# Another pool for a weight block, fewer eviction halves and other queues for some rows in a hybrid SSD and attention step

## The chip, the cores and the metric

The kernel runs on one core of a Trainium2 chip. The metric is the device time of one execution in microseconds (us); lower is better. A core has five engines: TensorE (PE in the profile, its weight loads PEld), VectorE (DVE), ScalarE (ACT), GpSimd (POOL, "Pool" below) and SyncE (SP), which here only issues DMAs. SP, ScalarE and Pool each have a queue of their own for the DMAs that they issue; each engine takes its instructions in order, so an instruction that waits holds all that stand behind it on that engine.

## The reference

One step of a one-layer decoder for 512 prompt tokens and 64 sample tokens (8 x 8). All matrices are float32.

```python
# h = rmsnorm(x); one input projection of h gives z, x/B/C, dt, q, k, v, ga, mix_s, mix_a
# attention:  o = sink_attention(q, k, v, rel_bias, window 128) * silu(ga)
# SSD:        y = grouped_rmsnorm(ssd(silu(conv(xBC)), dt) * silu(z))
# merge:      m = sigmoid(mix_s) * (y @ w_ssm) + sigmoid(mix_a) * (o @ w_attn)
# trunk:      out = final_rmsnorm(x + m @ w_out)
```

x has 576 rows of 2048, y has 4096 columns. The new caches of k and v (the old rows moved up by eight, and the new ones), the convolution's state and the SSM state are outputs too.

## The kernel before

Activations stand transposed, a tile of 128 features by T = 576 tokens, in two halves of TH = 288. Each float32 product is made as three products of rounded parts: `ah` and `al` are the high and low part of an activation, `wh` and `wl` those of a weight. A weight block is 128 x 8 x 128 (512 KB, "raw"); ScalarE rounds it to `wh` (L80) and VectorE takes the difference `wl` (L81).

**Two ways of multiplying.** `run_main` makes *single tiles*: 128 output columns from all sixteen feature tiles, two raw blocks each, loaded at L73. `pairs_of` makes *pairs* of output tiles by seven products instead of eight (Strassen's scheme in Winograd's form). Each pair takes four raw blocks (A11, A21, A22, A12, loaded at L380), and VectorE forms S1 = A21 + A22, S2 = S1 - A11, S3 = A11 - A21 and S4 = A12 - S2 out of them (L393). Each product is 24 matmuls of 288 columns. VectorE combines the products (L404) and names the halves p1, u, w, o, c.

**Stages** in the trace before: to about 122 us the norm, the transposes and the first six single tiles; in their shadow `sums_job` forms the combinations T of the activations that the products need. Then the paired run of 22 pairs for the gate columns (ga, z) to about 610, attention to about 1390, SSD to about 2335, the three *branch* products (w_attn, and w_ssm in two parts) to about 2975, and w_out. Each branch product is four single tiles (run_main), while `forms_job` loads the branch's rows once more and forms their combinations, and then six pairs. `merge_out` multiplies each half by its gate row `sg` (L1341 load, L1345 product) and stores it to `mg_d` by Pool (L1352 plain, L1350 adding to what is there).

**Pools in SBUF.** `wp` holds the raw blocks of single tiles, and of pairs A11 and A21, in two buffers. `rs` holds A22, A12, S1 and S2 in five buffers, and the staged rows ("stg") of `acts_in` and `forms_job`. `ev` holds halves of 128 x 288 (tag e), N_E = 14 of them: the halves of products, sums, gate rows, and `x` tiles.

**T1.** The combination T1 (x[0, 0] in `sums_job`) is needed in the buffers `b12`, which the first single tiles still read. So eight halves of `ev` keep it (the list t1) from `sums_job` until the first pair, when `t1_there` splits them into `b12`. At a branch T1 goes to the scratch `xb_d` (L1324) and is loaded from it (L1389) when the single tiles are issued.

**Order.** A scheduler places instructions on each engine by a simulated timeline, and a buffer of a pool is free for its next tile when the last reader of that one buffer is done. SP issues nearly all loads; Pool stores T1, b12 (`xb_d`) and `mg_d`, copies the two caches from DRAM to DRAM in `copy_job` (L529, eight DMAs of 480 KB), and writes the bias for attention to DRAM (L491, 16 DMAs of 383 KB). `acts_in` loads the rows for the single tiles of the next branch (L1309, on SP) and splits them (L1169 ScalarE, L1170 VectorE); `on_products` calls it during the last pair of a branch.

Of the kernel before, what the change touches and what calls it, by code (L numbers as in the profile page):

```python
# [16 lines left out]
P = 128  # L17
# [14 lines left out]
WIN = 128  # L32
EPS = 1e-6
NEG = -1e30
OFF_XBC = DI
OFF_DT = OFF_XBC + CONV
OFF_Q = OFF_DT + H
OFF_K = OFF_Q + D
OFF_V = OFF_K + KVW
# [13 lines left out]

Z_PAIRED = 28
FIRST_OUT = 4
N_E = 14
N_C = 18
N_K = 19

# [26 lines left out]
def hybrid(ctx, tc, x_prompt, x_sample, cache_k, cache_v, state_conv, state_ssm, norm_w, w_in, conv_w,  # L86
# [24 lines left out]
    def scratch(shape, name):  # L111
        return dram.tile(shape, F32, tag=name, name=name)
# [9 lines left out]
    ga_d = scratch([D, T], "ga_d")  # L122
    xb_d = scratch([D // 2, TH], "xb_d")
    mg_d = scratch([D, T], "mg_d")
    oh_d = scratch([HEADS * BL], "oh_d")
    ea_d = scratch([H, T], "ea_d")
    nacs_d = scratch([H, T], "nacs_d")
# [180 lines left out]
    def drain():  # L308
        while quick or jobs:
            pump()  # L310
# [55 lines left out]
    def pairs_of(w, r0, cols, ops, takes, after):  # L366

        n = len(cols)
        st = [{} for _ in cols]

        def load(p, *names):
            for x in names if p < n else ():
                c, kh = cols[p] + P * (x in ("A21", "A22")), x in ("A12", "A22")
                t_ = (rs if kh else wp).tile([P, 8, P], F32, tag="rs" if kh else "raw", name="raw",
                                             bufs=5 if kh else 2)
                sync.dma_start(out=t_, in_=w[r0 + 1024 * kh:r0 + 1024 * kh + 1024, c:c + P].rearrange("(k p) n -> p k n", p=P))  # L380
                st[p][x] = t_

        def sum_(p, x):
            if p >= n:
                return
            s_ = st[p]
            if x in ("S1", "S2"):
                s_[x] = rs.tile([P, 8, P], F32, tag="rs", name="raw", bufs=5)
            else:
                s_[x] = s_["A21" if x == "S3" else "S2"]  # L390
            a, b, op = {"S1": ("A21", "A22", ALU.add), "S2": ("S1", "A11", ALU.subtract),
                        "S3": ("A11", "A21", ALU.subtract), "S4": ("A12", "S2", ALU.subtract)}[x]
            vec.tensor_tensor(out=s_[x], in0=s_[a], in1=s_[b], op=op)  # L393

        def split(p, i):
            if p < n:
                st[p][i] = W.split(st[p][("A11", "S2", "S1", "S3", "A12", "S4", "A22")[i]])

        def evict(p, i):
            s_, (one, two) = st[p], takes[p]  # L400
            ps = s_["ps", i][:, :TH]

            def add(o, b):
                vec.tensor_tensor(out=o, in0=ps, in1=b, op=ALU.add)  # L404
                return o

            if i == 0:
                s_["p1"] = etile("p1")
                act.activation(s_["p1"], ps, AF.Copy)
            elif i == 1:  # L410
                s_["u"] = add(etile("u"), s_["p1"])
            elif i == 2:
                s_["w"] = add(etile("w"), s_["u"])
            elif i == 3:
                two(1, add(s_["w"], s_["w"]), s_["w"])
            elif i == 4:
                one(0, ps, etile("o"))
            else:
                c = add(etile("c"), s_["u"])
                (one if i == 5 else two)(1 if i == 5 else 0, c, c)  # L420

        def head():
            load(0, "A11", "A21", "A22", "A12")
            split(0, 0)
            sum_(0, "S1")
            sum_(0, "S2")
            split(0, 1)
            sum_(0, "S3")

        def run():  # L430
            for p in range(n):
                for i in range(7):
                    if i < 5:
                        split(p, i + 2)
                    else:
                        split(p + 1, i - 5)
                    if i == 1:
                        load(p + 1, "A11", "A21", "A22")
                    elif i == 2:
                        sum_(p, "S4")  # L440
                    elif i == 3:
                        sum_(p + 1, "S1")
                        load(p + 1, "A12")
                    elif i == 4:
                        sum_(p + 1, "S2")
                    elif i == 5:
                        sum_(p + 1, "S3")
                    st[p]["ps", i] = p1.tile([P, 512], F32, tag=f"ps{i}", name="ps") if i < 4 else st[p]["ps", (0, 2, 3)[i - 4]]
                    wh, wl = st[p].pop(i)
                    for k in range(8):  # L450
                        ah, al = ops[i][k]
                        for q, (a, b) in enumerate(((wh, ah), (wh, al), (wl, ah))):
                            ten.matmul(st[p]["ps", i][:, :TH], a[:, k, :], b, start=i < 4 and k == 0 and q == 0,  # L453
                                       stop=k == 7 and q == 2, skip_group_check=i >= 4)
                        pump()
                    evict(p, i)
                    after(p - n, i)

        return head, run
# [690 lines left out]
    def etile(name):  # L1150
        return ev.tile([P, TH], F32, tag="e", name=name)

    hx = [[[hb[k // 8][j][k % 8][part] for j in range(2)] for part in range(2)] for k in range(KT)]


    def pair_pools():
        stk = ExitStack()
        return (stk, *(stk.enter_context(tc.tile_pool(name=n_, bufs=b_, reuse_waits="tile"))
                       for n_, b_ in (("tx", 1), ("rs", 5), ("ev", N_E))))

    stk, tx, rs, ev = pair_pools()
    b12, t1 = hb[0][1], []
    ops = [hb[0][0], [], [], [], hb[1][0], hb[1][1], []]

    def tpair(tag):
# [7 lines left out]
    def sums_job():  # L1173

        yield from wait(36)
        for k in range(8):
            x = {}
            for i, j in ((0, 0), (0, 1), (1, 1), (1, 0)):
                x[i, j] = ev.tile([P, TH], F32, tag="e", name="x")
                vec.tensor_tensor(out=x[i, j], in0=hb[i][j][k][0], in1=hb[i][j][k][1], op=ALU.add)  # L1180
            pool.dma_start(out=xb_d[k * P:(k + 1) * P, :], in_=x[0, 1])
            for o_, a, b in (((0, 0), (0, 1), (0, 0)), ((0, 1), (1, 1), (0, 1)), ((1, 1), (1, 1), (0, 0)),
                             ((1, 0), (1, 0), (1, 1))):
                vec.tensor_tensor(out=x[o_], in0=x[a], in1=x[b], op=ALU.subtract)
                yield
            t1.append(x[0, 0])
            for i, o_ in ((3, (0, 1)), (1, (1, 1)), (6, (1, 0))):
                ops[i].append(split_half(tpair(f"t{i}{k}"), x[o_]))
                yield
# [6 lines left out]
            takes.append([gate_out(AF.Silu, dst, n + u) for u in range(2)])  # L1196
    back = []

    def t1_there():

        for k in range(8):
            split_half(b12[k], t1[k])

    def b12_again(p, i):
        if (p, i) == (-len(cols), 0):
            t1_there()
        elif (p, i) == (-1, 1):
            for k in range(8):
                back.append(etile("x"))
                sync.dma_start(out=back[k], in_=xb_d[k * P:(k + 1) * P, :])  # L1210
        elif (p, i) == (-1, 2):
            for k in range(8):
                split_half(b12[k], back[k])
# [3 lines left out]
    quick.append(sums_job())  # L1217
    run_main([m_in(c, by_halves(gate_out(AF.Sigmoid, d_, n))) for c, d_, n in mixes[:FIRST]], first, then=head)
    drain()
    ms.close()  # L1220
    ms = ExitStack()
    p1 = ms.enter_context(tc.tile_pool(name="p1", bufs=1, space=PSUM, reuse_waits="tile"))
# [53 lines left out]
    left = [m_in(n * P, take_gate(AF.Silu, z_d, n)) for n in range(Z_PAIRED, DI // P)] + left  # L1276
    seq = []
    for g in range(G):
        seq.append(m_in(OFF_XBC + (32 + g) * P, take_conv(32 + g)))
        seq.append(m_in(OFF_XBC + (40 + g) * P, take_conv(40 + g)))  # L1280
        for t in range(4):
            seq.append(m_in(OFF_XBC + (4 * g + t) * P, take_conv(4 * g + t) if t < 3 else last_x(g)))
        seq += left[:MIXES_S[g]]
        del left[:MIXES_S[g]]
    seq += left
# [15 lines left out]
    run_main([m_in(c, by_halves(gate_out(AF.Sigmoid, d_, n))) for c, d_, n in ends], raws=raws)  # L1301

    def staged_rows():
        return rs.tile([P, 8, P], F32, tag="rs", name="stg", bufs=5).rearrange("p a b -> p (a b)")

    def acts_in(src, ks):
        for k in ks:
            t_ = staged_rows()
            sync.dma_start(out=t_[:, :T], in_=src[k * P:(k + 1) * P, :])  # L1309
            split_half(hk[k], t_[:, :T])  # L1310

    tt = [[tpair(f"t{i}{k}") for k in range(8)] for i in (1, 3, 6)]
# [1 line left out]
    def forms_job(src):  # L1314

        for k in range(8):
# [4 lines left out]
            sync.dma_start(out=u2, in_=src[k * P:(k + 1) * P, TH:])  # L1321
            sync.dma_start(out=v[:, :T], in_=src[1024 + k * P:1024 + (k + 1) * P, :])
            vec.tensor_tensor(out=t1_, in0=u2, in1=u1, op=ALU.subtract)
            pool.dma_start(out=xb_d[k * P:(k + 1) * P, :], in_=t1_)  # L1324
            vec.tensor_tensor(out=t2_, in0=v2, in1=t1_, op=ALU.subtract)
            yield
            split_half(tt[0][k], t2_)
# [52 lines left out]
    for i in range(3):  # L1380
# [4 lines left out]
        def last_chunk():  # L1385
            head()
            for k in range(8):
                t1.append(etile("x"))
                sync.dma_start(out=t1[k], in_=xb_d[k * P:(k + 1) * P, :])  # L1389

        head, run = pairs_of(w, r0, [n * P for n in range(FIRST_OUT, KT, 2)], ops,
                             [takes[n:n + 2] for n in range(FIRST_OUT, KT, 2)],
# [157 lines left out]
```

## Time and profile before

| | us |
|---|---|
| median of 3 runs | 3226.87 (3225.44 to 3229.58) |
| the profiled execution | 3228.93 |
| its span, first to last instruction | 3226.8 |
| mean granted TensorE clock in it | 0.983 |

The costliest groups, by line: three matmul groups at L345 (single tiles and the rest of the run through `run_main`) of 1012 to 1021 us each, three at L453 (pairs) of 382 to 384 us each, VectorE's L81 with 728.0 us in 586 instructions, ScalarE's L80 with 620.1 us in as many.

How to read the lines below: a row of a timeline is the start in us, the duration, the engine, line, operation, out<-in by the program's names, and in brackets how long the engine had stood idle before, and what ended that. A row of the waits is who waited for whom: us in total, times, the longest. SPq is SP's own sequence of DMA issues. Names have no buffer numbers in the profile, so `t1_d` would read `t_d`.

### The profile page before, as it was taken

Reading aid. Unit: us, or ns where it says so; the run is one execution under the profiler, and the core shown is the slowest. Engines: PE = TensorE matmul, PEld = TensorE weight load, DVE = VectorE, ACT = ScalarE, POOL = GpSimd, SP = SyncE. Lnnn points to the kernel's source line nnn. Section 1 sums busy time; section 2 is a strip of 40 time slices with the busy share of each in tenths; the row PEclk is TensorE's granted clock in tenths of the full one; section 3 lists DMA queues with packets and bytes.
Section 4 is the critical chain, followed back from the end, with each engine's and each line's share of the span. In section 5 each row is a group of like instructions: output and inputs, shape, how many; then the busy total and the mean of one; then the engine's idle time right before and its main releaser. Section 6 shows DMA issues by size and latency. Waiting matters only on the chain. (4 is left out here: it accounts for less than half of the span.)

```text
span 3226.8 us, 58215 instructions
## 1 busy us (share of the span) xinstructions
PE 3112.4 (96%) x22939; PEld 2993.4 (93%) x22939; DVE 1996.5 (62%) x3434; ACT 1473.7 (46%) x2761; POOL 482.5 (15%) x591
## 2 busy tenths in 40 slices
PE   6989999999999999999999999999999999999997
PEld 5989999999898998999999999998899989998997
DVE  6656666515444443477687687686657777877354
ACT  5434444423554554455555555565433433434333
POOL 3200000000001010112213212212221031311111
PEclk9999999999999999999999999999999999999999
DMA  6564444433343243364464564565575676967655
GB/s 198 143 156 121 122 123 125 117 89 90 84 121 93 82 123 100 100 165 135 135 179 128 147 166 132 148 166 146 147 234 175 194 212 143 249 159 194 180 161 158
DMA packets 733650, 471.18 MB, mean 146 GB/s; under 512 B 45433, under 2 KB 696969, under 8 KB 733185
## 3 DMA queue, kind: packets, MB, share of 16 engines
q1 hardware_dynamic: 691616, 420.51, 46.6%
q0 software_dynamic: 24336, 29.20, 4.4%
q10 hardware_dynamic: 17424, 17.76, 1.7%
q8 instruction: 180, 2.95, 0.4%
q14 instruction: 94, 0.76, 0.1%
HBM read 385.79 MB, written 91.81 MB: 148 GB/s over the span
## 5 line engine op out<-in xcount | busy, mean ns | idle before, releaser
L80 ACT ACTIVATE wh<-raw 128x1024 fp32r<-128x1024 f32 x586 | 620.1, 1058 | 1031.6 <-PE ps L453 488.4
L81 DVE TENSOR_TENSOR wl<-raw,wh 128x1024 fp32r<-128x1024 f32 x586 | 728.0, 1243 | 529.9 <-ACT wh L80 525.9
L345 PE MATMUL ps<-ah,wh 128*128 128x288 f32 (+2 forms) x4384 | 1021.4, 302 | 34.8 <-ACT craw L828 10.1
L345 PE MATMUL ps<-ah,wl 128*128 128x288 f32 (+2 forms) x4384 | 1012.6, 301 | 3.5 <-DVE wl L81 3.3
L345 PE MATMUL ps<-al,wh 128*128 128x288 f32 (+2 forms) x4384 | 1012.4, 300 | 2.5 <-DVE al L1170 2.5
L345 PEld LDWEIGHTS ps<-ah,wh 128*128 128x128 f32 x4384 | 735.2, 192 | 50.5 <-issue 11.1
L345 PEld LDWEIGHTS ps<-ah,wl 128*128 128x128 f32 x4384 | 734.5, 191 | 19.6 <-issue 10.6
L345 PEld LDWEIGHTS ps<-al,wh 128*128 128x128 f32 x4384 | 734.6, 191 | 9.0 <-DVE al L1170 4.1
L453 PE MATMUL ps<-ah,wh 128*128 128x288 f32 x1280 | 382.2, 299 | 13.8 <-DVE w L404 5.6
L453 PE MATMUL ps<-ah,wl 128*128 128x288 f32 x1280 | 383.5, 300 | 5.9 <-DVE wl L81 5.4
L453 PE MATMUL ps<-al,wh 128*128 128x288 f32 x1280 | 381.8, 298 | 0.0
L453 PEld LDWEIGHTS ps<-ah,wh 128*128 128x128 f32 x1280 | 244.4, 191 | 14.7 <-issue 5.8
L393 DVE TENSOR_TENSOR raw<-raw 128x1024 f32<-128x1024 f32 x160 | 194.8, 1220 | 97.6 <-DMA raw<-in_w_in_dram 40.6
L453 PEld LDWEIGHTS ps<-ah,wl 128*128 128x128 f32 x1280 | 244.6, 191 | 9.3 <-DVE wl L81 9.2
L453 PEld LDWEIGHTS ps<-al,wh 128*128 128x128 f32 x1280 | 244.7, 191 | 0.1
L844 DVE SCALAR_TENSOR_TENSOR cacc<-craw,prm,cacc 128x600 f32<-128x600 f32 x144 | 126.8, 885 | 45.4 <-ACT cacc L842 43.7
L882 ACT ACTIVATE L<-L,nacs_n 128x128 f32<-128x128 f32 (+1 forms) x320 | 96.7, 379 | 56.6 <-DVE L L879 56.1
L610 DVE CUSTOM_DVE_ANT_0 sc<-bank,bm 128x256 f32<-128x256 f32 (+1 forms) x128 | 43.8, 388 | 80.0 <-PE bank L606 72.1
L923 POOL TENSOR_TENSOR xl<-xe,xh 128x512 fp32r<-128x512 f32 x32 | 58.6, 1832 | 200.3 <-ACT xh L922 199.9
L879 DVE TENSOR_TENSOR L<-L,nacs_n 128x512 f32<-128x512 f32 (+1 forms) x80 | 51.9, 662 | 47.7 <-DMA L<-nacs_d 47.3
L1093 DVE SCALAR_TENSOR_TENSOR s<-s,dec_s,bank 128x128 f32<-128x128 f32 x256 | 70.4, 340 | 10.3 <-PE bank L1087 9.3
L1241 POOL DMA_DIRECT2D dska<-in_d_skip_dram x1 | 0.6, 586 | 455.9 <-DMA z_d<-c 455.9
(575 smaller groups left out, 4497.7 us busy)
## 6 DMA issues: line engine op xcount, KB each, us to landing
raw<-in_w_in_dram SPq DMA_DIRECT2D x306, 512.0 KB
raw<-in_w_ssm_branch_dram SPq DMA_DIRECT2D x64, 512.0 KB
raw<-in_w_out_dram SPq DMA_DIRECT2D x64, 512.0 KB
L<-nacs_d SPq DMA_DIRECT2D x64, 256.0 KB
s<-in_state_ssm_dram SPq DMA_DIRECT2D x64, 256.0 KB
out_dram<-s SPq DMA_DIRECT2D x64, 256.0 KB
raw<-in_w_attn_branch_dram SPq DMA_DIRECT2D x32, 512.0 KB
stg<-y_d SPq DMA_DIRECT2D x48, 288.0 KB
```

The lines of the kernel that those rows point to most:

```text
L80: pin(nc.scalar.activation(wh, raw, AF.Copy))
L81: pin(nc.vector.tensor_tensor(out=wl, in0=raw, in1=wh, op=ALU.subtract))
L345: ten.matmul(sums[i][:, s, :part.shape[1]], a[:, kk, :], part, start=(k == 0 and q == 0), stop=(k == last and q == 2))
L393: vec.tensor_tensor(out=s_[x], in0=s_[a], in1=s_[b], op=op)
L453: ten.matmul(st[p]["ps", i][:, :TH], a[:, k, :], b, start=i < 4 and k == 0 and q == 0, stop=k == 7 and q == 2, skip_group_check=i >= 4)
L610: vec.tensor_tensor_reduce(out=s_[:, i, lo:256], in0=ps[:, i, lo:256], in1=bm[j][:, i, lo:256], scale=1.0, scalar=-3e38, op0=ALU.add, op1= ...
L844: vec.scalar_tensor_tensor(out=acc[:, :600], in0=raw[:, i:i + 600], scalar=prm[:, i * 48 + j:i * 48 + j + 1], in1=acc[:, :600], op0=ALU.mu ...
L879: vec.tensor_tensor(out=l_[:rows, :, :n], in0=l_[:rows, :, :n], in1=nacs_n[:rows, blk, h:h + 4].unsqueeze(2).to_broadcast([rows, 4, n]), o ...
L882: act.activation(l_[:rows, i, :n], l_[:rows, i, :n], AF.Exp, scale=-1.0, bias=nacs_n[:rows, blk, h + i:h + i + 1])
L923: pool.tensor_tensor(out=xl, in0=xe, in1=xh, op=ALU.subtract)
L1093: vec.scalar_tensor_tensor(out=sts[i][:, t, :], in0=sts[i][:, t, :], scalar=dec_s[:, 4 * g + t, b:b + 1], in1=ps[:, v, i, :], op0=ALU.mult ...
L1241: pool.dma_start(out=dska, in_=AP(d_skip, 0, [[0, P], [1, H]]))
```

## The change

1. A21 moves from the pool `wp` to `rs`, which gets a sixth buffer (5 to 6), through a helper `weights_tile`. `wp` keeps two buffers, for A11 and the single tiles. The loads for the next pair are written in the order A21, A22, A11 instead of A11, A21, A22.
2. `ev` shrinks from 14 halves to 11.
3. T1 of the first stage is stored to a new scratch `t1_d` by Pool and loaded into eight `ev` halves by SP after the first single tiles; the branches use `t1_d` too, instead of `xb_d`.
4. `acts_in` issues its loads from Pool's queue instead of SP's.

A renamed constant (OFF_XBC) has no effect. Lines shift by one to four (L1181 becomes L1184, L1309 L1313, L1341 L1345, L1350 L1354, L1352 L1356).

```diff
-N_E = 14
+N_E = 11
...
+    t1_d = scratch([D // 2, TH], "t1_d")
...
                 c, kh = cols[p] + P * (x in ("A21", "A22")), x in ("A12", "A22")
-                t_ = (rs if kh else wp).tile([P, 8, P], F32, tag="rs" if kh else "raw", name="raw",
-                                             bufs=5 if kh else 2)
+                t_ = weights_tile() if x != "A11" else wp.tile([P, 8, P], F32, tag="raw", name="raw", bufs=2)
...
             if x in ("S1", "S2"):
-                s_[x] = rs.tile([P, 8, P], F32, tag="rs", name="raw", bufs=5)
+                s_[x] = weights_tile()
...
                     if i == 1:
-                        load(p + 1, "A11", "A21", "A22")
+                        load(p + 1, "A21", "A22", "A11")
...
+    def weights_tile(name="raw"):
+        return rs.tile([P, 8, P], F32, tag="rs", name=name)
...
-                       for n_, b_ in (("tx", 1), ("rs", 5), ("ev", N_E))))
+                       for n_, b_ in (("tx", 1), ("rs", 6), ("ev", N_E))))
...
-            t1.append(x[0, 0])
+            pool.dma_start(out=t1_d[k * P:(k + 1) * P, :], in_=x[0, 0])
...
         if (p, i) == (-len(cols), 0):
-            t1_there()
+            for k in range(8):
+                split_half(b12[k], t1[k])
...
     drain()
+    for k in range(8):
+        t1.append(etile("x"))
+        sync.dma_start(out=t1[k], in_=t1_d[k * P:(k + 1) * P, :])
...
     def staged_rows():
-        return rs.tile([P, 8, P], F32, tag="rs", name="stg", bufs=5).rearrange("p a b -> p (a b)")
+        return weights_tile("stg").rearrange("p a b -> p (a b)")
...
             t_ = staged_rows()
-            sync.dma_start(out=t_[:, :T], in_=src[k * P:(k + 1) * P, :])
+            pool.dma_start(out=t_[:, :T], in_=src[k * P:(k + 1) * P, :])
...
-            pool.dma_start(out=xb_d[k * P:(k + 1) * P, :], in_=t1_)
+            pool.dma_start(out=t1_d[k * P:(k + 1) * P, :], in_=t1_)
...
-                sync.dma_start(out=t1[k], in_=xb_d[k * P:(k + 1) * P, :])
+                sync.dma_start(out=t1[k], in_=t1_d[k * P:(k + 1) * P, :])
```

**Pool's queue in the first stage.** Before, with the stores of `sums_job` (xb_d) and the copies of the caches (L529):

```order
24 L1181 DMA xb_d<-x 128x288
25 L1251 DMA sinks_s<-sink_d 64x4x1 x2
26 L529 DMA out_dram<-in_cache_k_dram 2x4x15360 x4
27 L529 DMA out_dram<-in_cache_v_dram 2x4x15360 x4
28 L1181 DMA xb_d<-x 128x288 x7
```

After, from the same place (t_d is t1_d), and then the rows that follow the writes of the bias:

```order
21 L1184 DMA xb_d<-x 128x288
22 L1189 DMA t_d<-x 128x288
23 L1184 DMA xb_d<-x 128x288
24 L1189 DMA t_d<-x 128x288
25 L1184 DMA xb_d<-x 128x288 x2
```

```order
41 L491 DMA bias_d<-oh_d 256x1x383 x16
42 L1245 DMA dska<-in_d_skip_dram 128x64
43 L1250 DMA sk<-in_attn_sinks_dram 32x1
44 L1247 COPY dsk<-dska 64x32 x2
45 L1252 COPY sk_6644<-sk 32x8
46 L1253 DMA sink_d<-sk_6644 32x8
47 L1255 DMA sinks_s<-sink_d 64x4x1 x2
48 L529 DMA out_dram<-in_cache_k_dram 2x4x15360 x4
49 L529 DMA out_dram<-in_cache_v_dram 2x4x15360 x4
```

The eight copies moved from behind the first xb_d store to behind dska, whose load waited until 633.28 us in the trace before; stores of T1 alternate with the other seven.

**SP's queue at the first pairs.** Before: raw_1259 to raw_1265 are A11, A21, A22 and A12 of pair 0 (the last two stand further ahead), raw_1448, 1450, 1452 and 1526 those of pair 1, raw_1690, 1692, 1694 and 1761 those of pair 2:

```order
23 L380 DMA raw_1259<-in_w_in_dram 128x8x128
24 L380 DMA raw_1261<-in_w_in_dram 128x8x128
25 L380 DMA raw_1452<-in_w_in_dram 128x8x128
26 L380 DMA raw_1448<-in_w_in_dram 128x8x128
27 L380 DMA raw_1450<-in_w_in_dram 128x8x128
28 L380 DMA raw_1526<-in_w_in_dram 128x8x128
29 L380 DMA raw_1694<-in_w_in_dram 128x8x128
```

After: raw_1268 is A11 of pair 0 (its other three stand ahead); raw_1473, 1475, 1477 and 1551 are A21, A22, A11 and A12 of pair 1, raw_1715 and 1719 A21 and A11 of pair 2, and raw_1954 A11 of pair 3. Between the two pieces stand the eight loads of T1 (L1223):

```order
22 L380 DMA raw_1268<-in_w_in_dram 128x8x128
23 L380 DMA raw_1473<-in_w_in_dram 128x8x128
24 L380 DMA raw_1477<-in_w_in_dram 128x8x128
25 L380 DMA raw_1719<-in_w_in_dram 128x8x128
```

```order
34 L380 DMA raw_1475<-in_w_in_dram 128x8x128
35 L380 DMA raw_1551<-in_w_in_dram 128x8x128
36 L380 DMA raw_1715<-in_w_in_dram 128x8x128
37 L380 DMA raw_1954<-in_w_in_dram 128x8x128
```

A22 of the next pair, which stood ahead of that pair's A11 and A21, is now the last of the four but A12; A11 stands two pairs ahead, and A21 of the pair after next stands right behind A12.

**Pool's queue at the end of the second branch.** Before, the last stores of the pairs and then the first of the forms:

```order
368 L1350 DMA mg_d<-w 128x288
369 L1350 DMA mg_d<-o 128x288
370 L1350 DMA mg_d<-c 128x288 x2
371 L1350 DMA mg_d<-w 128x288
372 L1350 DMA mg_d<-o 128x288
373 L1350 DMA mg_d<-c 128x288 x2
374 L1324 DMA xb_d<-stg 128x288
```

After, the same two pairs; L1313 are the rows for the next single tiles:

```order
384 L1313 DMA stg<-y_d 128x576
385 L1354 DMA mg_d<-w 128x288
386 L1354 DMA mg_d<-o 128x288
387 L1354 DMA mg_d<-c 128x288
388 L1313 DMA stg<-y_d 128x576
389 L1354 DMA mg_d<-c 128x288
390 L1313 DMA stg<-y_d 128x576 x7
391 L1354 DMA mg_d<-w 128x288
392 L1313 DMA stg<-y_d 128x576 x3
393 L1354 DMA mg_d<-o 128x288
394 L1313 DMA stg<-y_d 128x576 x4
395 L1354 DMA mg_d<-c 128x288 x2
```

Sixteen loads of rows stand between the stores of the last two pairs, fourteen of them around the last pair's, and none behind the last two stores. Ahead of w_out twelve of fourteen stand behind the last store.

More of the change, by code (lines that the diff above doesn't have):

```diff
@@ L34 @@
 NEG = -1e30
-OFF_XBC = DI
-OFF_DT = OFF_XBC + CONV
+OFF_xb_dC = DI
+OFF_DT = OFF_xb_dC + CONV
 OFF_Q = OFF_DT + H
@@ L1158, in pair_pools @@
         return (stk, *(stk.enter_context(tc.tile_pool(name=n_, bufs=b_, reuse_waits="tile"))
-                       for n_, b_ in (("tx", 1), ("rs", 5), ("ev", N_E))))
+                       for n_, b_ in (("tx", 1), ("rs", 6), ("ev", N_E))))
     stk, tx, rs, ev = pair_pools()
-    b12, t1 = hb[0][1], []
+    b12 = hb[0][1]
     ops = [hb[0][0], [], [], [], hb[1][0], hb[1][1], []]
@@ L1197, in hybrid @@
     back = []
-    def t1_there():
-        for k in range(8):
-            split_half(b12[k], t1[k])
+    t1 = []
     def b12_again(p, i):
         if (p, i) == (-len(cols), 0):
-            t1_there()
+            for k in range(8):
+                split_half(b12[k], t1[k])
         elif (p, i) == (-1, 1):
@@ L1278, in hybrid @@
     for g in range(G):
-        seq.append(m_in(OFF_XBC + (32 + g) * P, take_conv(32 + g)))
-        seq.append(m_in(OFF_XBC + (40 + g) * P, take_conv(40 + g)))
+        seq.append(m_in(OFF_xb_dC + (32 + g) * P, take_conv(32 + g)))
+        seq.append(m_in(OFF_xb_dC + (40 + g) * P, take_conv(40 + g)))
         for t in range(4):
-            seq.append(m_in(OFF_XBC + (4 * g + t) * P, take_conv(4 * g + t) if t < 3 else last_x(g)))
+            seq.append(m_in(OFF_xb_dC + (4 * g + t) * P, take_conv(4 * g + t) if t < 3 else last_x(g)))
         seq += left[:MIXES_S[g]]
```

## The prediction

> **What bounds the kernel now.** I read the page first, then the 25 us windows of the whole run, then the lists of waits and the timelines of those windows in which the matmuls fall short. The page says that TensorE is the bound nearly everywhere:
>
> ```profile
> PE 3112.4 (96%) x22939; PEld 2993.4 (93%) x22939; DVE 1996.5 (62%) x3434; ACT 1473.7 (46%) x2761; POOL 482.5 (15%) x591
> ```
>
> So a change that alters no matmul can win only where TensorE waits or runs at a low clock. The windows show where that is: x after PE is the matmuls that fell into the window, PEclk the granted clock, DMA the share of the 16 engines. The windows that matter:
>
> ```profile
> core 0: us, PE busy (x) PEld busy (x) DVE busy (x) ACT busy (x) POOL busy (x), PEclk, DMA share, GB/s
> 25.00:50.00 25.00, 23.61 (x156) 20.91 (x154) 22.88 (x57) 15.86 (x35) 13.60 (x15) 1.00 0.55 154
> 50.00:75.00 25.00, 19.55 (x128) 18.12 (x129) 17.49 (x46) 12.81 (x30) 1.71 (x3) 0.93 0.57 181
> 75.00:100.00 25.00, 25.00 (x190) 25.00 (x189) 19.75 (x45) 9.54 (x20) 2.16 (x4) 1.00 0.46 133
> 100.00:125.00 25.00, 25.00 (x190) 25.00 (x189) 17.21 (x29) 10.44 (x21) 2.51 (x5) 1.00 0.41 110
> ...
> 150.00:175.00 25.00, 22.43 (x158) 21.97 (x158) 12.89 (x14) 8.28 (x11) 8.45 (x8) 0.94 1.02 223
> 175.00:200.00 25.00, 18.08 (x120) 17.54 (x119) 12.25 (x14) 6.79 (x9) 1.05 (x1) 0.84 0.77 169
> 200.00:225.00 25.00, 25.00 (x180) 25.00 (x180) 15.75 (x17) 9.16 (x13) 0.00 (x0) 0.94 0.42 110
> ...
> 560.00:585.00 25.00, 25.00 (x191) 25.00 (x190) 17.76 (x19) 10.09 (x14) 0.00 (x0) 1.00 0.47 133
> 635.00:660.00 25.00, 25.00 (x193) 25.00 (x192) 4.90 (x4) 6.11 (x10) 0.41 (x2) 1.00 0.33 86
> ...
> 2575.00:2600.00 25.00, 20.91 (x153) 20.24 (x152) 19.36 (x31) 9.74 (x19) 11.92 (x16) 0.98 0.86 265
> 2600.00:2625.00 25.00, 24.24 (x161) 24.04 (x162) 17.32 (x27) 9.44 (x17) 11.81 (x15) 0.88 0.97 271
> 2625.00:2650.00 25.00, 22.51 (x157) 22.10 (x156) 19.43 (x28) 10.04 (x16) 3.42 (x4) 0.93 0.69 168
> 2700.00:2725.00 25.00, 24.32 (x183) 24.08 (x182) 17.80 (x23) 7.77 (x9) 3.72 (x5) 1.00 0.64 147
> 2825.00:2850.00 25.00, 22.16 (x147) 21.95 (x146) 20.22 (x28) 9.50 (x15) 3.43 (x4) 0.86 0.72 181
> 2975.00:3000.00 25.00, 17.10 (x86) 14.79 (x84) 10.69 (x24) 6.65 (x10) 0.00 (x0) 0.83 1.05 329
> ```
>
> A full window holds 190 matmuls, so one is 25 / 190 = 0.132 us, a product of 24 is 3.16 us and a pair of seven products 22.1 us. What a window is short of 190, times 0.132, is its loss, slow clock included. 560 to 585 stands for the paired run after 225: nothing is lost there, and no earlier weight load can help it. The losses are 12.7 us at 25 to 75 (34 and 62 matmuls), 14.7 us at 150 to 225 (32, 70 and 10), 13.0 us at 2575 to 2650 (37, 29, 33), and 13.7 us at 2975 to 3000 (104). The third branch's start, of which only the last row (43 short, 5.7 us) is shown, is of the second's kind. The change touches each of these places.
>
> **Start: the cache copies leave Pool's queue.** Before, eight copies of 480 KB stand between the first and the second xb_d store (timelines of Pool, DVE and PE; what ended the idle time is in brackets):
>
> ```profile
> 40.91 2.19 POOL L529 DMA_DIRECT2D out_dram<-in_cache_k_dram  x4
> 43.09 2.13 POOL L529 DMA_DIRECT2D out_dram<-in_cache_v_dram  x4
> 55.10 0.59 POOL L1181 DMA_DIRECT2D xb_d<-x  x1 [9.87 <-DMA out_dram<-in_cache_k_dram]
> 61.91 0.95 DVE L1184 TENSOR_TENSOR x<-x 128x288 f32<-128x288 f32 x2 [5.48 <-DMA xb_d<-x]
> 63.66 0.80 PE L345 MATMUL ps<-ah,wh 128*128 128x288 f32 x4 [2.21 <-ACT ah L236]
> 69.98 0.85 PE L345 MATMUL ps<-ah,wh 128*128 128x288 f32 x2 [2.80 <-ACT o L1137]
> ```
>
> The store waits 9.87 us for a copy, VectorE then 5.48 us for that store, and TensorE stands idle 2.21 and 2.80 us soon after, with a clock of 0.93 in the window (0.07 x 25 = 1.75 us). That is 6.8 us that can hang on the copies. In the new order they stand behind dska, in the attention stage. I take 4 us, somewhat over half: both waits of TensorE name ScalarE, which may be late for reasons of its own. Upper bound: the whole second window, 8.2 us. Lower bound: the change puts eight t1_d stores into the same stretch of Pool's queue; at the 0.59 us of the xb_d store they are 4.7 us of issuing, and were all of it in VectorE's path, the term would be -4.7.
>
> The copies go to about 633 us. The window from 635 has a DMA share of 0.33 and full TensorE, and Pool issues little there. Eight issues are 4.3 us of Pool by the two rows above. Cost 0, covered by that idle share; without the cover they could cost again what they cost now, 6.8 us.
>
> **T1 by way of scratch.** Eight loads on SP bring T1 back before the third product of pair 0 (the pairs start near the end of the window 100 to 125). They wait for their stores, of which the last leaves in the first stage, and for buffers that ScalarE's stores of the last single tiles free. The window 100 to 125 is full at a DMA share of 0.41: cost 0. If they were late, everything behind them on SP, A22 of pair 1 first, would be late too; a store and a load are each some 4 us (the median landing of mg_d stores, below), so up to 4 us lost; early they bring nothing.
>
> **Paired run: a sixth rs buffer, and A21 a pair ahead.** The loss at 150 to 225 is a weight that comes late under the bias_d writes. From the DVE timeline, PE's waits, and the DMA issues of 120 to 210:
>
> ```profile
> 192.99 1.23 DVE L393 TENSOR_TENSOR raw<-raw 128x1024 f32<-128x1024 f32 x1 [11.13 <-DMA raw<-in_w_in_dram]
> ...
> PE ps L453 <- DVE w L404: 5.6, 1, 5.6
> ...
> raw<-in_w_in_dram SPq DMA_DIRECT2D x12, 512.0 KB
> bias_d<-oh_d POOLq DMA_DIRECT2D x16, 383.0 KB, 22.0
> ```
>
> Sixteen writes of 383 KB are in flight for 22 us each while twelve weight blocks are fetched, and a VectorE sum waits 11.13 us for one. The evictions queue behind that sum (w L404), and TensorE behind them. The change cannot thin the writes. It only puts the weights further ahead: seven raw buffers become eight, and A21 of the next pair waits for the split of an old A22 instead of that of S3. A pair uses four blocks, so one block is 22.1 / 4 = 5.5 us of TensorE. I take 5.5 us. Bounds: 14.7 us (all of it) above; below, A22 is now the late load, waiting for the split of S1; were it later by one product than the load that it replaces as the last, it would be -3.2 us.
>
> **Branch pairs with 11 halves.** Each half that leaves needs a gate row sg, loaded into one of the ev buffers; three fewer means that its load waits for an mg_d store of a half that went before, and that weight loads stand behind it on SP. The steady rows of the second branch:
>
> ```profile
> 2698.81 1.89 SPq L380 DMA_DIRECT2D raw<-in_w_ssm_branch_dram  x2
> 2700.80 1.61 SPq L1341 DMA_DIRECT2D sg<-ms_d  x2
> 2706.53 0.46 DVE L1345 TENSOR_TENSOR c<-c,sg 128x288 f32<-128x288 f32 x1 [3.49 <-DMA sg<-ms_d]
> ```
>
> VectorE already waits 3.49 us for sg, behind two weight loads, and TensorE loses 7 matmuls (0.9 us) in that window. In the new order sg and weights alternate singly, which helps; fewer buffers hurt. I take 0; bounds: +0.9 us for each of the 12 pairs of the last two branches (11 us), and the same lost.
>
> **Rows for single tiles from Pool's queue.** The second branch's start, by the waits of PE, SP and POOL, and by Pool's timeline:
>
> ```profile
> PE ps L345 <- ACT t33h L1169: 3.7, 1, 3.7
> SPq L1309 <- DVE wl L81: 8.6, 4, 5.4
> mg_d<-o POOLq DMA_DIRECT2D x10, 144.0 KB, 4.2
> 2563.82 0.54 POOL L1352 DMA_DIRECT2D mg_d<-w  x1 [9.79 <-DVE w L1345]
> 2575.18 0.54 POOL L1352 DMA_DIRECT2D mg_d<-c  x1 [7.98 <-DVE c L1345]
> ```
>
> SP stands 8.6 us at rows that wait for weight splits (L1309); weight and gate loads behind them now go ahead, and the sixth rs buffer stages one row more. Against that, the DMA engines are 0.86 to 0.97 busy there, so a transfer that starts earlier slows another, and TensorE's longest wait is for a table of the forms (t33h), whose loads stay on SP. Of the 13.0 us of this start and the 5.7 us shown of the third I take 4. Bounds: 13 us above, one start's whole loss; below, a row behind an mg_d store on Pool: 9.8 us at one start.
>
> The Trainium skill, "DMA: Bandwidth & Descriptors", section "Issuing engines are not separate DMA queues", speaks against this part: transfers from any engine share the same 16 DMA engines, and another issuer saves only the issuing. The rows of 0.86 and 0.97 agree. By that rule this term would be near 0 and the time 3214; the 8.6 us that SP waits, which is not issuing, speak for more.
>
> **End: w_out.** The last rows on SP and the chain of waits:
>
> ```profile
> 2964.68 4.71 SPq L1309 DMA_DIRECT2D stg<-mg_d  x5
> 2974.94 1.18 SPq L1422 DMA_DIRECT2D res<-in_x_prompt_dram  x2
> 2975.38 9.59 DMA res<-in_x_prompt_dram
> 2985.04 13.26 DMA raw<-in_w_out_dram
> 2998.38 1.06 ACT wh L80
> ```
>
> The chain is a w_out block that takes 13.26 us under the loads of res, at a DMA share of 1.05. In the new order one w_out block stands one res load earlier, and the rows no longer hold SP, so res can start before 2974. Half a megabyte at the window's 329 GB/s is 1.6 us; with an earlier start of res I take 3. Bounds: 8 us above (the 9.59 us of res in the chain less one load); below, 12 rows at Pool's 0.54 us instead of SP's (4.71 us for five, waits within) and behind the last mg_d stores, 5 us lost.
>
> **Sum.** 4 + 5.5 + 0 + 4 + 3 = 16.5 us. The profiled execution took 3228.93 us (span 3226.8), so it would be 3212.4. The median of the runs lies 2.1 us lower, at 3226.87, and gives **3210**, which I forecast: 0.5% faster. 0.2% (6.5 us) is about what a measurement of this kernel can tell from no change.
>
> **Rivals.**
> - *Bytes, not order, bind* at the bias writes and the branch starts: the DMA share of 1.02 at 150 to 175 and 0.97 at 2600 to 2625 speak for it, the drop to 0.77 while VectorE waits longest (175 to 200) against. Then 5.5 and 4 fall away, and the start loses half to the t1_d stores: 2 + 3 = 5 us, 3222. Chance 0.18, within 0.2%.
> - *Rows stuck in Pool's queue.* Pool takes its queue in order, and mg_d stores wait up to 9.79 us for VectorE. Rows that stand behind the last of them come only when the last products have been combined, while the single tiles of the next branch wait for them; and stores that stand behind rows free their ev halves late: 9.8 us at each of two branch starts and at the end, 29 us, less the 9.5 us of the first two terms: slower by 20, 3247. It decides once the rows that stand behind the last stores are needed sooner than some 10 us after them. Against it: at the branch starts all rows stand ahead of the last two stores; only at the end do twelve stand behind the last. Chance 0.10.
> - *Gate rows starve.* With 11 halves each branch pair's sg comes 3.5 us later than now (a second wait of the size above). VectorE is idle 7.2 us of 25, so it takes one such wait at 0.9 us of TensorE and about half of a second: 18 x 1.75 = 31 us less 16.5: 3242. It decides where VectorE's idle time is used up, some 6.4 us per pair. Against it: before, loads of weights rather than buffers set when sg came. Chance 0.09.
> - The rest, 0.63, is the forecast: 3196 to 3219.
>
> Range, 8 in 10: up into the first slower case, 3232, and down to where two terms come near their upper bounds (4 more at the start, 9 more at the bias writes), 3195. Faster by over 0.2%: 0.64; within: 0.17; slower: 0.19.
>
> **What would show it.** Start: no VectorE wait of 5 us for xb_d at 60, and 140 matmuls or more at 50 to 75. Bias writes: L393's waits for raw fall from 11 us to some 6, and 150 to 225 loses about 9 us. Attention: 635 to 685 full in spite of a higher DMA share. Branch pairs: 183 or more in each steady window; wrong, if SP's waits at sg grow and PE waits for wl. Branch starts: rows issued by Pool before 2580, and no PE wait for ah; wrong, if Pool's rows come after its last mg_d store and ah waits for them. End: over 100 matmuls in the window of w_out's start. I would be wrong most of all if the paired run after 225, full now, lost anything.

## The result and the profile after

| | us |
|---|---|
| before, median of 8 runs | 3226.15 (3221.20 to 3231.49) |
| changed, median of 8 runs | 3238.83 (3231.94 to 3249.96) |
| ratio changed / before, 95% interval | 1.0042, 1.0024 to 1.0061 |
| changed, the profiled execution (its span) | 3248.36 (3246.5) |

The change makes the kernel slower by 0.4%. The forecast was 3210, faster by 0.5%, in a range of 3195 to 3232. The profiled execution of the changed kernel lies 9.5 us above its median, so its losses below are somewhat large. One execution of all those below, of e8, ran at a granted clock of 0.856 and took 3377.90 us; it is left out of e8's number.

The windows of the changed kernel that answer to those of before (same columns):

```profile
25.00:50.00 25.00, 23.15 (x132) 20.97 (x132) 18.91 (x48) 12.29 (x29) 8.01 (x5) 0.93 0.34 95
50.00:75.00 25.00, 21.50 (x146) 19.89 (x147) 21.33 (x52) 15.49 (x36) 3.22 (x6) 0.93 0.34 94
150.00:175.00 25.00, 14.98 (x100) 14.74 (x99) 9.38 (x11) 4.97 (x7) 9.37 (x9) 0.80 1.21 172
175.00:200.00 25.00, 19.57 (x133) 19.34 (x133) 7.93 (x8) 6.46 (x9) 1.05 (x1) 0.86 0.96 210
200.00:225.00 25.00, 22.90 (x162) 22.67 (x161) 18.73 (x22) 9.13 (x12) 0.00 (x0) 0.93 0.40 109
650.00:675.00 25.00, 23.39 (x177) 23.16 (x176) 4.90 (x4) 5.37 (x10) 5.33 (x10) 1.00 0.69 222
2575.00:2600.00 25.00, 25.00 (x190) 25.00 (x189) 21.41 (x31) 15.53 (x22) 10.64 (x18) 1.00 0.97 310
2600.00:2625.00 25.00, 25.00 (x190) 25.00 (x189) 23.43 (x38) 9.23 (x20) 16.11 (x22) 1.00 0.90 264
2700.00:2725.00 25.00, 23.25 (x176) 22.98 (x175) 16.23 (x20) 7.72 (x8) 3.43 (x4) 1.00 0.58 131
2725.00:2750.00 25.00, 21.46 (x151) 21.23 (x150) 16.59 (x20) 6.93 (x8) 3.43 (x4) 0.93 0.57 133
```

The second branch's start, short before, is full at 2575 to 2625, and 50 to 75 has 146 matmuls instead of 128 (though 25 to 50 has 132 instead of 156). But the pairs behind it, nearly full before (183 at 2700), fall to 151, the bias writes cost more (100 at 150 to 175), and the cache copies leave a mark at 650.

Windows shift when a kernel gets later. Each kernel has the same 22,939 matmuls, so I set the start of the n-th matmul in one trace against the n-th in the trace of before, and read at stage borders how far the one had moved. Below, each number is what a stage added to the time (us, minus is faster; places by the time in the trace before; one execution each). The SSD stage orders its matmuls otherwise in most of the kernels, so a number there holds for the stage as a whole only; and a border that falls on a pause, as 2452 does, can move up to 1.3 us from one row to the next. The rows left out add 0.3 us at most (660 to 687) and -3.5 to +0.5 (after 3014). The labels are those of the experiments:

```
                           after      e6      e8      e1      e2     e10      e3     e11     e13     e12     e14     e15     e16
start to 115                -0.5    -3.6    -3.9    -1.6    -2.0    -2.6    -4.8    -5.9    +0.2    -5.7    -5.3    -4.9    -6.2
115 to 217                  +8.4   +10.9   +10.3    +1.0    +4.6    +6.5    +7.1    +1.4    -2.0    +4.1    -2.0    +1.5    -2.8
217 to 660                  +2.1    +2.2    +2.3    +0.3    -0.0    +2.4    +1.9    +2.1    +0.1    +2.0    +2.2    +2.3    +2.4
687 to 1881                 -0.4    -4.0    -3.0    +0.1    -5.9    -3.8    -6.1    -2.4    -2.6    -4.0    -4.6    -4.2    -3.7
1881 to 2358                +9.2    +6.0    +5.4    +2.4    +1.0    +0.2    +1.7    +0.5    +0.3    +5.7    +6.1    +0.3    +1.0
2358 to 2452 start 1        -3.8    -3.6    -5.0    +1.5    -1.2    -5.0    -5.9    -5.6    -1.1    -6.6    -7.0    -6.6    -4.6
2452 to 2564 pairs 1        +2.3    +2.0    +0.5    +1.2    +0.3    +1.1    +1.0    +0.9    -0.2    -0.2    -0.2    -0.2    -0.2
2564 to 2644 start 2        -8.5    -7.3    -5.3    -2.7    -2.1    -6.2    -3.8    -3.0    -4.1    -6.2    -7.0    -5.7    -8.2
2644 to 2766 pairs 2        +9.2    +7.3    +4.0    -1.8    +3.3    +0.2    +1.7    +0.9    -3.5    -3.5    -3.5    -3.5    -3.5
2766 to 2846 start 3        -3.1    -4.6    -6.4    +6.2    +0.7    -5.1    -3.4    -6.0    -4.7    -4.6    -5.1    -6.1    -5.4
2846 to 2962 pairs 3        +7.0    +6.5    +7.9    +1.7    +0.7    -0.6    -0.4    +2.9    -3.7    -3.8    -3.7    -3.7    -3.7
2962 to 3014 w_out          -1.8    -0.7    -3.6    +3.7    -0.8    -0.3    -0.3    +0.2    -1.7    -3.0    -4.0    -1.7    -2.6
```

In the column "after" the starts of the branches and of w_out win 17.2 us, the branch pairs lose 18.5, the bias writes 8.4, and the stretch from 1881 to 2358 loses 9.2.

**Who waits in the pairs.** PE's and VectorE's waits of the changed kernel at 2640 to 2770, and VectorE's timeline there (SP issued a weight block at 2722.20):

```profile
PE ps L453 <- DVE wl L81: 8.2, 5, 3.5
PE ps L453 <- DVE o L1349: 3.9, 2, 2.3
...
DVE raw L393 <- issue: 12.4, 3, 4.8
DVE c L1349 <- DMA sg<-ms_d: 10.7, 4, 3.9
DVE raw L393 <- DMA raw<-in_w_ssm_branch_dram: 7.9, 2, 4.2
...
2728.48 1.23 DVE L393 TENSOR_TENSOR raw<-raw 128x1024 f32<-128x1024 f32 x1 [4.79 <-issue]
2729.62 0.45 DVE L404 TENSOR_TENSOR u<-ps,p 128x288 f32<-128x288 f32 x1
2729.99 1.21 DVE L393 TENSOR_TENSOR raw<-raw 128x1024 f32<-128x1024 f32 x1
2731.12 1.22 DVE L81 TENSOR_TENSOR wl<-raw,wh 128x1024 fp32r<-128x1024 f32 x1
...
2732.39 0.47 PE L453 MATMUL ps<-ah,wl 128*128 128x288 f32 x1 [3.54 <-DVE wl L81]
```

L393 at 2728.48 is S1 of the *next* pair. VectorE stands 4.79 us before it, and behind it stand u and then the split of A12 of the pair that *runs* (L81 at 2731.12), for which TensorE then waits 3.54 us. The waits for gate rows (10.7 us) are no longer than before. The same place in the kernel before, in the windows of the second branch:

```profile
2691.92 1.23 DVE L393 TENSOR_TENSOR raw<-raw 128x1024 f32<-128x1024 f32 x1 [3.12 <-issue]
2693.06 0.45 DVE L404 TENSOR_TENSOR w<-ps,u 128x288 f32<-128x288 f32 x1
```

There S1 stood one product later, behind u and the split of A12 and with w behind it, and its wait of 3.12 us held TensorE little: in 2650 to 2750 of that trace TensorE's wait for splits is the first line below. The lines after it are, from the pages, TensorE's second matmul group of all pairs of the run, before and changed, with its idle time at the end:

```profile
PE ps L453 <- DVE wl L81: 0.9, 2, 0.7
...
L453 PE MATMUL ps<-ah,wl 128*128 128x288 f32 x1280 | 383.5, 300 | 5.9 <-DVE wl L81 5.4
L453 PE MATMUL ps<-ah,wl 128*128 128x288 f32 x1280 | 384.7, 301 | 33.6 <-DVE wl L81 33.4
```

With A21 in `rs` the scheduler put S1 ahead of u and of the split of A12. That it did so because the block comes earlier in its simulated timeline is inferred; that timeline is not on record.

An early S1 alone does not cost. In the paired run after 225 of the changed kernel S1 stands just as early in nearly all pairs, but its waits are shorter there (225 to 600 below, 2.6 us the longest), and TensorE loses nothing:

```profile
DVE raw L393 <- DMA raw<-in_w_in_dram: 18.5, 17, 2.6
...
217.00:642.00 425.00, 425.00 (x3211) 425.00 (x3210) 286.62 (x308) 174.31 (x236) 1.09 (x2) 1.00 0.43 121
```

### The profile page after: what moved, and what is told of

Its sections match the earlier page's. It is cut to its first block, busy times and chain, and to the rows that moved or that the text cites. A ratio compares the mean times of both kernels' runs of the same rounds, so it can differ in the third digit from the quotient of the medians.

```text
span 3246.5 us, 58237 instructions
## 1 busy us (share of the span) xinstructions
PE 3119.8 (96%) x22939; PEld 2999.4 (92%) x22939; DVE 2004.6 (62%) x3434; ACT 1473.4 (45%) x2763; POOL 513.2 (16%) x661
## 5 line engine op out<-in xcount | busy, mean ns | idle before, releaser
L81 DVE TENSOR_TENSOR wl<-raw,wh 128x1024 fp32r<-128x1024 f32 x586 | 726.8, 1240 | 570.9 <-ACT wh L80 567.9
L453 PE MATMUL ps<-ah,wl 128*128 128x288 f32 x1280 | 384.7, 301 | 33.6 <-DVE wl L81 33.4
L393 DVE TENSOR_TENSOR raw<-raw 128x1024 f32<-128x1024 f32 x160 | 195.2, 1222 | 110.3 <-DMA raw<-in_w_in_dram 49.5
```

The source lines that it names most:

```text
L81: pin(nc.vector.tensor_tensor(out=wl, in0=raw, in1=wh, op=ALU.subtract))
```

## The experiments

Each number is a median of several runs (four to ten), with the ratio to the kernel before, run beside it, and its 95% interval.

**e1, the rows from Pool's queue alone** (on the kernel before).

```diff
-            sync.dma_start(out=t_[:, :T], in_=src[k * P:(k + 1) * P, :])
+            pool.dma_start(out=t_[:, :T], in_=src[k * P:(k + 1) * P, :])
```

> The kernel before with one part alone: the rows for single tiles come from Pool's queue. In the traces of before and after the stretch of each branch start got shorter by 3.8, 8.5 and 5.6 us and w_out's start by some 2. Theory R (the queue did that): this kernel is faster than before by 12 to 20 us, about 3210. Rival S (the sixth rs buffer did it, more staged rows at a time): within 4 us of before, and the branch starts lose as before.

3230.36 us, 1.0019 (1.0007 to 1.0031). R falls: no gain. The table has +6.2 and +3.7 at the third start and w_out.

**e2, T1 by scratch and 11 halves alone** (on the kernel before).

```diff
-N_E = 14
+N_E = 11
...
-            t1.append(x[0, 0])
+            pool.dma_start(out=t1_d[k * P:(k + 1) * P, :], in_=x[0, 0])
...
```

> The kernel before with T1 by way of scratch and 11 eviction halves; five rs buffers, A21 in its old pool, rows from SP. After lost some 21 us in the six pairs of each of the three branches. Theory G (gate rows starve with 11 halves): the branch pairs lose 15 to 20 us here too, about 3243. Theory O (the order of the loads, with A22 last and the sum S1 early in VectorE's sequence): branch pairs as before, 3222 to 3230.

3227.32 us, 1.0004 (0.9993 to 1.0014). G falls: the branch pairs lose 4.3 us in all.

**e3, A21 back in its old pool and order** (on the changed kernel).

```diff
-                t_ = weights_tile() if x != "A11" else wp.tile([P, 8, P], F32, tag="raw", name="raw", bufs=2)
+                t_ = weights_tile() if kh else wp.tile([P, 8, P], F32, tag="raw", name="raw", bufs=2)
...
-                        load(p + 1, "A21", "A22", "A11")
+                        load(p + 1, "A11", "A21", "A22")
```

> The changed kernel with A21 back in the raw pool and the loads in the old order A11, A21, A22; six rs buffers, 11 halves, T1 by scratch and rows from Pool's queue stay. Theory O: the 8.5 us lost at the bias writes and the 21 us of the branch pairs are gone, the gain at the branch starts stays, 3208 to 3214. Theory G: only the 8.5 us are gone, about 3230.

3216.83 us, 0.9972 (0.9962 to 0.9982): faster than before. A21's move alone costs 22 us. The branch pairs lose 2.3 us instead of 18.5 and the starts keep 13 us; but 7.1 of the 8.4 us at the bias writes stay, so they have another cause than O named.

**e6, 14 halves in the changed kernel.**

```diff
-N_E = 11
+N_E = 14
```

> The changed kernel with 14 eviction halves. Theory G: the 21 us of the branch pairs come back, about 3218, while the bias writes still cost 8 us more than before. Theory O: no change against the changed kernel, 3234 to 3244.

3238.18 us, 1.0043 (1.0026 to 1.0060), as the changed kernel. Three halves more change nothing; with e2 this settles G.

**e12, S1 held at its place in the program** (on the changed kernel; the call puts an instruction behind all that were written ahead of it on its engine).

```diff
-            vec.tensor_tensor(out=s_[x], in0=s_[a], in1=s_[b], op=op)
+            ins = vec.tensor_tensor(out=s_[x], in0=s_[a], in1=s_[b], op=op)
+            if x == "S1":
+                tc.keep_in_program_order(ins)
```

> The changed kernel with one thing different: the sum S1 of the next pair keeps its place in the program on VectorE, behind the split of A12 and the combination w of the pair that runs; pools and loads as changed. In the changed kernel the scheduler puts S1 one product earlier, ahead of that split, where VectorE waits for A22 and holds the split. Theory O1 (S1's wait stands in the way of the splits): the branch pairs recover as with A21 in its old pool, 3212 to 3222. Theory O2 (A22 is loaded too late, wherever S1 stands): as the changed kernel, 3234 to 3244.

3202.26 us, 0.9925 (0.9907 to 0.9943). O1 holds, by more than it expected: 37 us off the changed kernel with the pools and the written order of the loads untouched. Between the two profiled executions, 46 us apart, the table puts 26.0 us in the branch pairs and 4.3 at the bias writes; the rest lies at the start, in the SSD stage and elsewhere, and what S1's place does there was not traced. TensorE's idle time before the group of 33.6 us above falls to nothing (first line below, from the page). Its VectorE and PE in the pairs, from the timeline and the windows, follow:

```profile
L455 PE MATMUL ps<-ah,wl 128*128 128x288 f32 x1280 | 377.0, 295 | 0.0
...
2718.31 0.45 DVE L406 TENSOR_TENSOR u<-ps,p 128x288 f32<-128x288 f32 x1
2719.09 1.23 DVE L81 TENSOR_TENSOR wl<-raw,wh 128x1024 fp32r<-128x1024 f32 x1 [0.33 <-ACT wh L80]
2721.33 0.46 DVE L406 TENSOR_TENSOR w<-ps,u 128x288 f32<-128x288 f32 x1 [1.01 <-PE ps L455]
2722.29 1.23 DVE L81 TENSOR_TENSOR wl<-raw,wh 128x1024 fp32r<-128x1024 f32 x1 [0.50 <-ACT wh L80]
2723.43 1.22 DVE L393 TENSOR_TENSOR raw<-raw 128x1024 f32<-128x1024 f32 x1
...
2700.00:2725.00 25.00, 25.00 (x191) 25.00 (x190) 19.04 (x24) 8.36 (x9) 3.41 (x4) 1.00 0.63 152
2725.00:2750.00 25.00, 25.00 (x191) 25.00 (x191) 18.99 (x26) 11.03 (x14) 8.52 (x14) 1.00 0.62 158
```

S1 (L393) comes behind the splits and starts with no wait at all; the pairs are full.

**e8, the old order of the loads, A21 still in rs.**

```diff
-                        load(p + 1, "A21", "A22", "A11")
+                        load(p + 1, "A11", "A21", "A22")
```

> The changed kernel with the loads for the next pair in the old order A11, A21, A22; A21 stays in the rs pool. S1 still stands ahead of the combination u and the split of A12 on VectorE. O1: slow as the changed kernel, 3232 to 3244. O2 (order of the loads): 3212 to 3222.

3237.07 us, 1.0035 (1.0022 to 1.0047). The order of the loads is not it; with A21 in rs the scheduler puts S1 early in either order.

**e10, e3 with the rows back on SP's queue** (the diff of e1, reversed).

> The kernel with six rs buffers and A21 in its old pool that took 3217, but with the rows for single tiles on SP's queue. If Pool's queue gives the gain at the branch starts: 3226 or more. If the sixth rs buffer gives it, as the rows alone (3230) suggest: 3210 to 3220.

3215.99 us, 0.9961 (0.9949 to 0.9974), as e3. The branch starts win 16.3 us without Pool's queue: the sixth rs buffer does it. e2 is this kernel with five buffers; its branch starts win 2.6 us, and it takes 3227.32 us.

**e11, six buffers and the rows from Pool, T1 kept in 14 halves** (on the kernel before).

```diff
-                       for n_, b_ in (("tx", 1), ("rs", 5), ("ev", N_E))))
+                       for n_, b_ in (("tx", 1), ("rs", 6), ("ev", N_E))))
...
-            sync.dma_start(out=t_[:, :T], in_=src[k * P:(k + 1) * P, :])
+            pool.dma_start(out=t_[:, :T], in_=src[k * P:(k + 1) * P, :])
```

> The kernel before with two parts: six rs buffers and the rows from Pool's queue. T1 stays in 14 eviction halves, without stores and loads by scratch. If the scratch route (later chain of the bias, eight loads on SP) costs the 7 us that every kernel with it and six buffers lost at the bias writes: 3209 to 3213. If those 7 us come from the six buffers, or differ from run to run: 3215 to 3220.

3212.49 us, 0.9952 (0.9936 to 0.9967). Beside e3 the scratch route, with its 11 halves, costs 4.3 us; in the table the difference lies at the bias writes (+1.4 against +7.1).

**e13, S1 held in the kernel before** (the diff of e12).

> The kernel before with one thing different: S1 keeps its place in the program on VectorE. It stood behind the split of A12 and ahead of the combination w already, so the wait moved little. If S1's place was what A21's move spoiled: little changes here, 3220 to 3230. If holding S1 back helps whatever the pools are: 3205 to 3215, and the changed kernel's parts have no share in the 3202.

3205.94 us, 0.9941 (0.9927 to 0.9956). The second expectation: the kernel before lost some 20 us to S1's place already, and the change made it worse. Of the 23 us between the two profiled executions 7.4 lie in the branch pairs and 9.9 in the three starts, where S1 of a branch's first pair is held too; why the starts gain was not traced.

**e15 and e14: S1 held in e3 (A21 in its old pool), and S1 held with A21 in rs but T1 kept in 14 halves.**

> The kernel with six rs buffers, 11 halves and A21 back in its old pool (3217), with S1 kept in its place. If A21's new pool is worth something once S1 waits at its old place (the load starts earlier): slower than 3202 by 4 us or more, 3207 to 3217. If not: 3200 to 3205.

> S1 kept in its place, A21 in the rs pool of six buffers, rows from Pool's queue, but T1 kept in 14 eviction halves as before, no scratch. The scratch route cost about 4 us at the bias writes (3216.8 with it, 3212.5 without, both without S1 held). If that adds to the rest: 3196 to 3200. If S1's place covers it: 3201 to 3204.

e15: 3192.96 us, 0.9899 (0.9885 to 0.9914), faster than both expectations. A21's new pool costs 9 us even with S1 held (3202 against 3193); in the table 5.4 of it lie between 1881 and 2358 and 2.6 at the bias writes. e14: 3194.69 us, 0.9908 (0.9892 to 0.9925), below its expectation; the scratch route and its 11 halves cost 7.6 us there, 6.1 at the bias writes.

**e16, six buffers, the rows from Pool, S1 held; A21 and T1 as before** (e11 with the diff of e12).

> S1 kept in its place, six rs buffers, rows from Pool's queue; A21 in its old pool and T1 kept in 14 eviction halves. The kernel of 3193 has T1 by scratch and 11 halves, the kernel of 3195 A21 in the rs pool. If both parts cost a few us each also with S1 held: 3186 to 3191, the fastest. If S1's place and the sixth buffer are all that counts: 3192 to 3196.

3187.61 us, 0.9882 (0.9856 to 0.9909): the fastest, 1.2% below the kernel before.

## Why the prediction was wrong, point by point

**The step that failed** is the pair of terms on the order of the loads: "I take 5.5 us" at the bias writes and "I take 0" for the branch pairs (+8.4 and +18.5 us in the profiled run). They asked when a block arrives. What counted was where on VectorE the sum that reads it stands. An instruction that waits holds all behind it on its engine, and the change moved the waiting S1 from behind the split of A12 to ahead of it. The order of VectorE's instructions showed this move before any run; I listed the loads on SP and not the sum that waits for them. Shown by e12 and e8: S1's place changed and the time changed by 37 us, with the branch pairs full; the written order of the loads changed and the time did not. A second term failed with it: T1 by way of scratch, taken at 0.

**Branch pairs (0 forecast, +18.5 measured in the profiled run).** The bounds, 11 us for two branches, were too small too, and the loss priced there, from too few halves for the gate rows, was not at work (e6, e2). The hint stood in a view of before that I did not quote:

```profile
DVE c L1345 <- DMA sg<-ms_d: 15.2, 4, 3.9
DVE raw L393 <- issue: 12.8, 4, 3.7
```

In 2650 to 2750 of the kernel before, S1 waited 12.8 us in four times, nearly as much as the gate rows did. "issue" means that the profile names no releaser, not that nothing is waited for; S1 reads two fetched blocks, and other rows of L393 do name a load (7.9 us in the changed kernel's list above). I read the sg row and passed over the other. The prediction would be "wrong most of all" if the paired run after 225 lost anything; it lost nothing, so that part held.

**Bias writes (-5.5 forecast, +8.4 measured).** Here VectorE's row of the changed kernel is

```profile
166.34 1.23 DVE L393 TENSOR_TENSOR raw<-raw 128x1024 f32<-128x1024 f32 x1 [13.68 <-DMA raw<-in_w_in_dram]
...
PE ps L453 <- DVE wl L81: 17.5, 3, 10.0
```

against 11.13 us for the longest wait before. A block further ahead did not help, since its sum stood further ahead too: TensorE now waits 17.5 us for splits, 10.0 of them behind this S1 (the rest is behind later sums that wait for their blocks in the same way), and with S1 held (e12) the stage loses 4.3 us less. The scratch route, which I had at 0 with up to 4 us lost if its loads were late, is the larger part: kernels that differ in it and the halves alone differ by 5.7 us (e3, e11), 6.1 (e12, e14) and 4.3 (e15, e16) here. Why it costs so much was not tried. The reason that the prediction gave for its bound, A22 of pair 1 late behind the loads of T1, fits the order but is not shown: in the changed kernel SP is done with the eight loads only near 118 us, and A22 of pair 1 goes behind them.

**Start (-4 forecast).** Right in kind: VectorE's wait of 5.48 us for xb_d is gone, and the kernels in which the copies left the start are 2.6 to 6.2 us earlier at 115, the changed kernel's profiled run alone only 0.5 (those that kept them there: 2.0 earlier to 0.2 later). The copies leave the start in every kernel with six rs buffers and in none with five (e1, e13, and e2, which has the new stores of T1), so this gain and the next loss come with the sixth buffer. **Copies (0 forecast): 2 us.** All kernels with the copies in the attention stage (at 634 to 655) lose 1.9 to 2.4 us by 660, those without them 0.3 at most. An idle DMA share was no full cover: ScalarE waits 9.7 us for a weight while the copies, 14 us each, are in flight:

```profile
ACT wh L80 <- DMA raw<-in_w_in_dram: 12.0, 2, 9.7
out_dram<-in_cache_k_dram POOLq DMA_DIRECT2D x4, 480.0 KB, 14.0
```

**Branch starts and end (-7 forecast, -17.2 measured).** The branch starts win 15.4 us where I had 4, w_out 1.8 where I had 3. The sign was right, the size of the starts far too small, and the main reason the wrong one: e1 has Pool's queue and no gain, e10 the sixth buffer, which I named only beside it, and the gain. The right sign was in part luck. The rule of the Trainium skill, "DMA: Bandwidth & Descriptors", section "Issuing engines are not separate DMA queues", that I set aside because of SP's 8.6 us of waits, held: e3 (3216.8) and e10 (3216.0) differ in the queue alone.

**Rivals.** Rows stuck in Pool's queue did not decide the result, though e1's losses at the third start and at w_out (+6.2, +3.7) lie where that rival put them; starving gate rows are refuted (e6, e2). My slower cases had a chance of 0.19 in all, and none held the mechanism.

**Open.** The stretch from 1881 to 2358, in the SSD stage, loses 5.4 to 9.2 us in all five kernels with A21 in rs and 0.2 to 2.4 in the others. No pair runs there. The order of the instructions differs in that stage from kernel to kernel; which of them loses the time was not tried.

## What to carry to other kernels

Where a scheduler orders by a simulated timeline, moving a load's buffer can pull its reader forward on an in-order engine, ahead of work that the running step needs, and where that reader's wait is long (up to 4.8 us in the branch pairs, 2.6 in the paired run, which lost nothing) the step waits too; look up the reader's new place, not only the load's. Give an instruction that waits for a transfer a place behind the work that must not wait: here that one line was worth 20 us on the old kernel and 37 on the new one. Test the parts of a change by themselves: this one held a gain (the sixth buffer) and two losses (A21's pool, the scratch route).

## What the runs showed of the hardware

- In-order engines pass a wait on: VectorE stood 4.79 us before a sum that waited for a load, and TensorE then waited 3.54 us for a split that stood behind it. In the pairs of the whole run TensorE's idle time before the matmuls that need a `wl` was 5.9 us before, 33.6 in the changed kernel, and 0.0 there with the sum held behind the split.
- A DMA share of 0.33 in a stretch did not hide eight copies of 480 KB put there: every kernel with them lost 1.9 to 2.4 us.
- The spread of a kernel's runs does not follow these waits plainly: 3231.94 to 3249.96 us over eight runs of the changed kernel and 3200.65 to 3203.81 over four with S1 held (e12), but 3209.46 to 3212.89 over five runs of e11, where S1 was not held.
